# Off-diagonal blocks of the chunk inverses made for two chunks at a time, and new priorities for the mixers

## The chip, the cores and the metric

The kernel runs on one core of a Trainium2 chip. The metric is the device time of one execution in microseconds (us). In the profile PE is TensorE's matrix product, PEld its weight load, DVE is VectorE, ACT ScalarE, POOL GpSimd and SP SyncE, which issues the transfers.

## The reference

One inference step of a decoder trunk of two layers, for a prompt of 16 + 512 rows and 8 sample rows, all in float32. Each layer is a half-step feed-forward block, a mixer and a second half-step feed-forward block:

```python
x = x + 0.5 * _swiglu(_rmsnorm(x, p['norm_ffn1'][l]), p['ffn1_w_in'][l], p['ffn1_w_out'][l])
h, s_w, s_s, s_c = _mixer(_rmsnorm(x, p['norm_mix'][l]), ...)
x = x + h
x = x + 0.5 * _swiglu(_rmsnorm(x, p['norm_ffn2'][l]), p['ffn2_w_in'][l], p['ffn2_w_out'][l])
```

The mixer's core is a recurrence over the rows, per head, with a 64 x 64 state (16 heads), beside a short convolution and two gates:

```python
Sa = jnp.einsum('bhvk,bhk->bhv', S, a_t)
S = S * w_t[:, :, None, :] + Sa[..., None] * b_t[:, :, None, :] + v_t[..., None] * k_t[:, :, None, :]
y = jnp.einsum('bhvk,bhk->bhv', S, r_t)
```

## The kernel before

The 536 columns (528 prompt rows and 8 sample rows) lie along the free dimension, the 1024 features over 8 tiles of 128 partitions. Each large product is split into three float32r products (high by high, high by low, low by high; `mm3`), with the weights split when they are loaded: `raw` by DMA, `hi` by ScalarE, `lo` by VectorE (`load_split`). Their accumulators are called `acc`, `a`, `x`, `y`, `z`, `ag` and `au`.

The mixer takes the recurrence in 11 chunks (NC) of 48 rows (C), for two heads at a time: 8 head pairs p in each layer. In a chunk, a unit lower triangular 48 x 48 matrix is inverted for each head. `stage_k(p)` makes the keys' side: projections, two low-rank products (`lora`), decays with a scan (`cum`), norms (`kq`, `kql`, `wn`), the Gram products (`wg`) and the inverses. The diagonal blocks of 24 rows (HC) are inverted on POOL by 23 steps of two operations (`pr`, `Xinv`) over a tile `Ta`, which comes through DRAM (`td`), and go through DRAM (`xd`) into the tile `Yd`. The off-diagonal block of each chunk is then made on TensorE by three operations of 48 x 48 per chunk: a transpose (w1, lines 1061 to 1077), a product with `off`, the off-diagonal block (w2), and a product with the inverse of the lower block (w3). They go in two halves of 6 and 5 chunks (SPL), each through one PSUM bank (tag c0 or c1 by the pair's parity), with a copy out by ScalarE after every step. The trace calls all of these tiles w: w<-cst,Yd is w1, w<-x,off is w2 and w<-Yd,x is w3. LATE (4 us) delays w1's operations in the plan.

`stage_v(p)` makes the values' side (`wv`, `wg`, `wp`), `chain(p)` steps through the 11 chunks one after the other with five TensorE operations each (all named cq), in the same bank as the pair's inverse, and `gnorm(p)` normalizes (`wm`). `stage_m(p)` and `merged(p)` gate and split the result. `gated_parts` are 40 projections and their elementwise work, which `fill` hands out between the stages by the list `gated`. `sample()` makes the 8 sample rows' recurrence in 8 blocks, each with a state tile in the buffers of `Ta` (line 1335). In the tail of the mixer the first half of the output product (`mh`, `ml`) is made.

All instructions go through a planner (`Sched`), which builds each engine's order when the kernel is built: an operation's priority is its place in the program less the `boost` of its stage (MIX, one set for each layer: k, v, c, g, m, i, s and w for stages, f for gated parts, e for the copies out of projections, h for weight loads ahead). Each has a price by `price` (lines 142 to 161); the planner takes the ready operation of the highest priority. `vector` in MIX lists the elementwise operations that VectorE makes; POOL makes the others. Since every operation is issued by one line, the trace gives L273 for all of them, and they are told apart by their tiles.

Of the kernel before, what the change touches and what calls it, by code (L numbers as in the profile page):

```python
# [7 lines left out]
F32 = mybir.dt.float32  # L8
F32R = mybir.dt.float32r
AF = mybir.ActivationFunctionType  # L10
# [5 lines left out]
P = 128  # L16
# [15 lines left out]
C = 48  # L32
NC = L // C
HC = C // 2
D = 64
# [3 lines left out]
RW = C + D  # L39
NH = 16  # L40

MIX = [dict(boost={'k': 600, 'v': 2000, 'c': 2000, 'g': -1500, 'f': -1000, 'm': -1000, 's': -1000, 'i': 2000, 'w': -6000, 'e': 0, 'h': 0},
            ka=4, gated=[0, 2, 0, 0, 0, 1, 1, 1, 0, 0, 2, 1, 0, 1, 1, 2, 0, 1, 2, 1, 0, 0, 0, 1, 2, 2, 0, 0, 2, 1, 0, 0],
            same=3000, inv=(),
            vector=('bv', 'ka', 'kh', 'kql', 'kt', 'm', 'mb', 'rk', 'rnip', 'rt', 's1', 's3a', 'sl', 'u', 'yl', 'zg')),
       dict(boost={'k': 1500, 'v': -1000, 'c': 2000, 'g': 100, 'f': -3000, 'm': -50, 's': 1000, 'i': 1500, 'w': 50, 'e': -2000, 'h': -2000},
            ka=4, gated=[0, 3, 0, 0, 1, 0, 0, 1, 1, 0, 2, 2, 1, 0, 0, 1, 0, 0, 1, 4, 1, 0, 1, 0, 1, 1, 0, 1, 1, 1, 0, 0],
            same=0, inv=(),
            vector=('bv', 'kh', 'kql', 'kt', 'm', 'mb', 'rk', 'rt', 's3a', 'sl', 'u', 'yl', 'zg'))]
LATE = 4.0  # L50
SHARE = 0.7
FIRST = -300
# [47 lines left out]
class Sched:  # L100
# [41 lines left out]
    def price(self, eng, fn, out, ins, kw):  # L142
        n = self.width(out)
        if fn == "dma_start":
            return 0.48, 4 * n * out.shape[0] / self.DMA_RATE
        if eng == "tensor":
            if fn == "transpose" or kw.get("is_transpose"):
                return n / 1200 + 2e-3, self.HOP
            return (max(n, 256) / 2400 + 12e-3 if ins[0].dtype == F32R else n / 600 + 6e-3), self.HOP
        if eng == "vector":  # L150
            if fn == "memset":
                return 8e-3 + n / 960, self.HOP
            if fn == "reciprocal":
                return 0.12 + n * 6.16e-3, self.HOP
            if fn == "tensor_reduce":
                n = self.width(ins[0])
            return (0.15 if len(ins) > 2 else 0.09) + n / 960, self.HOP
        if eng == "scalar":
            psum = any(x.tensor.space == PSUM for x in ins + [out])
            return (0.05 if psum else 0.095) + (0.09 if "scale" in kw else 0) + n / 1200, self.HOP  # L160
        return (0.28 + n * 1.7e-3 if fn == "tensor_tensor" else 0.2 + n * 1e-3), self.HOP
# [198 lines left out]
class Build:  # L360
# [423 lines left out]
    def mixer(self, l, xh, xl, mD):  # L784
        tc, nc, io, cst, R = self.tc, self.nc, self.io, self.cst, self.R
        V, G, A, T, S = nc.vector, nc.gpsimd, nc.scalar, nc.tensor, nc.sync
# [3 lines left out]
        boost, ka = opt['boost'], opt['ka']  # L790
        self.ahead = boost['h']
        E = lambda n: V if n in opt['vector'] else G
        with ExitStack() as ctx:
# [19 lines left out]
            o, _ = _PC["mu"]  # L813
            V.tensor_scalar(out=omu, in0=self.par[l][:, o:o + 26], scalar1=-1.0, scalar2=1.0, op0=ALU.mult, op1=ALU.add)
            nkk = pp.tile([P, 8], F32, name="nkk")
            o, _ = _PC["kk"]
# [41 lines left out]
            for i in range(2):  # L858
                t = pp.tile([P, NC, 2 * C], F32, name=f"Yd{i}")
                G.memset(t, 0.0)  # L860
                yds.append(t)
            off = pp.tile([P, NC, C], F32, name="off")
            G.memset(off, 0.0)

            def mname(c):
                return "mask" if c % 2 == 0 else "mask2"
# [71 lines left out]
            def stage_k(p):  # L938
# [91 lines left out]
                for g in range(4):  # L1030
                    S.dma_start(out=td[g].rearrange("c s t -> s c t"), in_=GT[g * HC:(g + 1) * HC])
                NP, HJ = 88, HC // 2
                Ta = pp.tile([P, HC, HC], F32, tag="Ta", name="Ta", bufs=2)
                for q in range(2):
                    for b in range(2):
                        o = (2 * q + b) * 22
# [17 lines left out]
                    rw = slice(g * HC, (g + 1) * HC)  # L1054
                    S.dma_start(out=Yd[rw, :, rw], in_=xd[g].rearrange("c j t -> j c t"))
                for h in range(2):
                    rw = slice(h * HC, (h + 1) * HC)
                    S.dma_start(out=off[rw, :, rw], in_=td[h, :, :, HC:].rearrange("c s t -> s c t"))
                    S.dma_start(out=Yd[rw, :, C + h * HC:C + (h + 1) * HC], in_=xd[2 + h].rearrange("c j t -> j c t"))

                for c0, c1 in SPL:
                    n = c1 - c0
                    x1, x2 = (pp.tile([P, 6 * C], F32, tag="tH", name=t, bufs=3)[:C, :n * C].rearrange("p (c q) -> p c q", c=n)
                              for t in ("x1", "x2"))

                    def step(fn, out, name):
                        w = psp.tile([P, 512], F32, tag=f"c{p % 2}", name=name, bufs=1)
                        for i in range(n):
                            fn(w[:C, i * C:(i + 1) * C], c0 + i)
                        A.activation(out=out, in_=w[:C, :n * C].rearrange("p (c q) -> p c q", c=n), func=AF.Copy)  # L1070

                    nc.pad = LATE
                    step(lambda o, c: T.transpose(o, Yd[:C, c, :C], cst["id"][:C, :C]), x1, "w1")
                    nc.pad = 0.0
                    step(lambda o, c: T.matmul(out=o, lhsT=off[:C, c, :], rhs=x1[:, c - c0, :], start=True, stop=True), x2, "w2")
                    step(lambda o, c: T.matmul(out=o, lhsT=x2[:, c - c0, :], rhs=Yd[:C, c, C:], start=True, stop=True),
                         Yd[:C, c0:c1, C:], "w3")

                nc.boost = boost['k']
                kf, kh, rk = a, k, r  # L1080
# [193 lines left out]
            def sample():  # L1274
# [57 lines left out]
                bv_ = lambda i: VB[:, i, :].unsqueeze(1).to_broadcast([P, SV, D])  # L1332
                for q in range(D // SV):
                    vs = slice(q * SV, (q + 1) * SV)
                    stf = pp.tile([P, HC * HC], F32, tag="Ta", name="s2", bufs=2)[:, :SV * D]
                    st = stf.rearrange("p (a b) -> p a b", a=SV)
                    S.dma_start(out=stf, in_=io["swkv"][l][:, q * SV * D:(q + 1) * SV * D])
                    t1 = tmp("t1")[:, :SV * D].rearrange("p (a b) -> p a b", a=SV)
                    E('s1').tensor_tensor(out=t1, in0=st, in1=bv_(3), op=ALU.mult)
                    V.tensor_reduce(out=sa[:, vs], in_=t1, op=ALU.add, axis=AX.X)  # L1340
                    E('sw').tensor_tensor(out=st, in0=st, in1=bv_(0), op=ALU.mult)
                    t2 = tmp("t2")[:, :SV * D].rearrange("p (a b) -> p a b", a=SV)
                    E('s2').tensor_tensor(out=t2, in0=bv_(4), in1=sa[:, vs].unsqueeze(2).to_broadcast([P, SV, D]), op=ALU.mult)
                    E('s2a').tensor_tensor(out=st, in0=st, in1=t2, op=ALU.add)
                    t3 = tmp("t3")[:, :SV * D].rearrange("p (a b) -> p a b", a=SV)
                    E('s3').tensor_tensor(out=t3, in0=bv_(1), in1=VB[:, 2, vs].unsqueeze(2).to_broadcast([P, SV, D]), op=ALU.mult)
                    E('s3a').tensor_tensor(out=st, in0=st, in1=t3, op=ALU.add)
                    S.dma_start(out=io["o_sswkv"][l][:, q * SV * D:(q + 1) * SV * D], in_=stf)
                    t4 = tmp("t4")[:, :SV * D].rearrange("p (a b) -> p a b", a=SV)
                    E('s4').tensor_tensor(out=t4, in0=st, in1=bv_(5), op=ALU.mult)  # L1350
                    V.tensor_reduce(out=y[:, vs], in_=t4, op=ALU.add, axis=AX.X)
# [267 lines left out]
```

## Time and profile before

| | us |
|---|---|
| median of 3 runs | 2955.64 (2954.28 to 2958.29) |
| the profiled execution | 2957.18 |
| its span, first to last instruction | 2955.4 |

| engine | busy us | share of the span |
|---|---|---|
| PE | 2873.6 | 97% |
| PEld | 2811.0 | 95% |
| DVE | 2135.9 | 72% |
| ACT | 1362.6 | 46% |
| POOL | 587.7 | 20% |

The feed-forward blocks take the span from 0 to 390, from 1110 to 1840 and from 2575 on; the mixers lie between them. A busy PE contains records that overlap: what a group of records costs is read from the starts of the records before and behind it, not from their durations.

### The profile page before, as it was taken

What the parts mean: (1) busy time and instruction counts of PE and PEld (TensorE: products, weight loads), DVE (VectorE), ACT (ScalarE), POOL (GpSimd) and SP (SyncE); (2) the same over time, 40 slices, a digit from 0 to 9 for tenths busy, and PEclk for the clock granted to TensorE, in tenths of its full rate; (3) what the DMA queues carried; (4) which work ended last, traced back from release to release, by engine and by line L of the source; (5) the groups of instructions that cost most, each with busy time, mean ns of one, the idle gap of its engine ahead of it and who ended that gap; (6) DMA issues with size and microseconds to landing.
All of it is one profiled execution on the core that took longest, in us unless ns stands there. A gap on an engine that the chain in (4) does not pass through costs nothing.

```text
span 2955.4 us, 57453 instructions
## 1 busy us (share of the span) xinstructions
PE 2873.6 (97%) x23026; PEld 2811.0 (95%) x23026; DVE 2135.9 (72%) x3995; ACT 1362.6 (46%) x2284; POOL 587.7 (20%) x1120
## 2 busy tenths in 40 slices
PE   8999999999999899999999999999999999999998
PEld 8999999999999899999999999999899998899997
DVE  8677767677776968676687766667766768687775
ACT  5444454344444245444454444535454442554444
POOL 1000026222342800000100001343430428100001
PEclk9999999999999989999999999999999999999999
DMA  3223323232323362323323333232232234623332
GB/s 133 93 96 98 112 87 92 74 86 83 87 64 99 130 207 87 104 90 104 108 71 101 100 94 116 90 96 78 62 84 75 62 103 139 214 79 108 96 102 80
DMA packets 219516, 294.22 MB, mean 100 GB/s; under 512 B 119824, under 2 KB 128784, under 8 KB 219248
## 3 DMA queue, kind: packets, MB, share of 16 engines
q1 hardware_dynamic: 219248, 290.54, 32.0%
q8 instruction: 181, 2.97, 0.4%
q14 instruction: 87, 0.71, 0.1%
HBM read 256.38 MB, written 34.10 MB: 98 GB/s over the span
## 4 chain that ended last, share of the span: by engine, by line
PE 86%; DVE 6%; ACT 2%; DMA 2%; issue 2%; POOL 1%; SPq 0%; DVEq 0%; ACTq 0%; POOLq 0%
PE acc L273 26%; PE a L273 17%; PE x L273 13%; PE y L273 7%; PE cq L273 5%; PE wg L273 3%; PE au L273 3%; PE z L273 3%; PE ag L273 3%; PE w L273 2%; DVE lo L273 2%; PE wp L273 2%; DMA raw<-in_f_in 1%; ACT hi L273 1%; POOL t L273 1%
## 5 line engine op out<-in xcount | busy, mean ns | idle before, releaser
L273 ACT ACTIVATE hi<-raw 128x1024 fp32r<-128x1024 f32 (+4 forms) x460 | 388.5, 845 | 488.6 <-PE acc L273 190.4
L273 DVE TENSOR_TENSOR lo<-raw,hi 128x1024 fp32r<-128x1024 f32 (+4 forms) x460 | 449.3, 978 | 58.0 <-ACT hi L273 52.2
L273 PE MATMUL acc<-xh,hi 128*128 128x268 f32 (+1 forms) x2112 | 481.3, 301 | 6.8 <-ACT sig L273 2.2
L273 PE MATMUL acc<-xh,lo 128*128 128x268 f32 (+1 forms) x2112 | 482.3, 301 | 5.5 <-DVE lo L273 5.4
L273 PE MATMUL acc<-xl,hi 128*128 128x268 f32 (+1 forms) x2112 | 478.2, 299 | 0.0
L273 PEld LDWEIGHTS acc<-xh,hi 128*128 128x128 f32 x2112 | 343.6, 192 | 12.5 <-ACT sig L273 3.3
L273 PEld LDWEIGHTS acc<-xh,lo 128*128 128x128 f32 x2112 | 343.6, 192 | 10.9 <-DVE lo L273 8.8
L273 PEld LDWEIGHTS acc<-xl,hi 128*128 128x128 f32 x2112 | 343.1, 191 | 1.1
L273 PE MATMUL a<-hh,lo 128*128 128x268 f32 (+1 forms) x1408 | 288.0, 285 | 0.9 <-DVE lo L273 0.9
L273 PE MATMUL a<-hl,hi 128*128 128x268 f32 (+1 forms) x1408 | 287.3, 285 | 0.0
L273 PE MATMUL a<-hh,hi 128*128 128x268 f32 (+1 forms) x1408 | 286.7, 285 | 0.0
L273 POOL MEMSET wide<- 128x104 f32 (+1 forms) x7 | 1.3, 188 | 1327.4 <-DVE s L273 945.8
L273 PE MATMUL x<-xh,hi 128*128 128x268 f32 (+1 forms) x864 | 247.3, 286 | 1.4 <-ACT sn L273 1.2
L273 PE MATMUL x<-xl,hi 128*128 128x268 f32 (+1 forms) x864 | 247.1, 286 | 0.0
L273 PE MATMUL x<-xh,lo 128*128 128x268 f32 (+1 forms) x864 | 246.9, 286 | 0.0
L273 ACT ACTIVATE hi<-s 128x1024 fp32r<-128x1024 f32 x144 | 152.0, 1057 | 185.8 <-DVE s L273 121.8
L273 PEld LDWEIGHTS a<-hh,lo 128*128 128x128 f32 x1408 | 219.6, 188 | 1.1 <-DVE lo L273 1.1
L273 PEld LDWEIGHTS a<-hl,hi 128*128 128x128 f32 x1408 | 218.6, 188 | 0.0
L273 PEld LDWEIGHTS a<-hh,hi 128*128 128x128 f32 x1408 | 218.6, 188 | 0.0
L273 DVE TENSOR_TENSOR lo<-s,hi 128x1024 fp32r<-128x1024 f32 x144 | 174.6, 1220 | 19.6 <-ACT hi L273 18.7
L273 POOL TENSOR_TENSOR pr<-Ta,Xinv 88x22 f32<-88x22 f32 (+16 forms) x368 | 149.6, 407 | 146.9 <-DMA Ta<-td 122.2
L273 DVE SCALAR_TENSOR_TENSOR X<-a,X 128x536 f32<-128x536 f32 (+1 forms) x160 | 113.0, 707 | 74.4 <-PE a L273 74.2
(570 smaller groups left out, 7204.3 us busy)
## 6 DMA issues: line engine op xcount, KB each, us to landing
raw<-in_f_in SPq DMA_DIRECT2D x176, 512.0 KB
raw<-in_w_in SPq DMA_DIRECT2D x132, 512.0 KB
raw<-in_f_out SPq DMA_DIRECT2D x128, 256.0 KB
raw<-in_f_out SPq DMA_DIRECT2D x32, 384.0 KB
raw<-in_w_o SPq DMA_DIRECT2D x32, 256.0 KB
XD<-X SPq DMA_DIRECT2D x16, 268.0 KB
s<-in_swkv SPq DMA_DIRECT2D x16, 256.0 KB
out_o_sswkv<-s SPq DMA_DIRECT2D x16, 256.0 KB
```

The lines of the kernel that those rows point to most:

```text
L273: return getattr(getattr(self.nc, o.eng), o.fn)(*o.args, **o.kw)
```

## The change

The transposes are made for an even chunk and the odd one after it together: the odd chunk's upper inverse stands beside the even one's in `Yd`, so one transpose of 48 x 96 puts the two below each other. `off` becomes block diagonal for two chunks (96 x 96, six of them), so one product of K = 96 makes w2 for both, and a new tile `xb` holds the lower inverses of two chunks as a block diagonal, so one product with 96 moving columns makes w3 for both. The eleventh chunk stays single. w1 and w2 are made for all chunks in one bank, w3 in two halves as before. `xb` and `off` are filled by four transfers each, `Yd`'s second half by two. `Ta` has one buffer instead of two, and the sample's state alternates between it and `xb`.

Beside it the planner's prices of transposes, of small float32 products and of scans change, and in MIX the boosts, the gated counts, layer 1's `same` and which operations VectorE makes. Only blank lines are left out of the changed code:

```diff
--- before.py
+++ after.py
@@ -39,14 +39,14 @@
 RW = C + D
 NH = 16
 
-MIX = [dict(boost={'k': 600, 'v': 2000, 'c': 2000, 'g': -1500, 'f': -1000, 'm': -1000, 's': -1000, 'i': 2000, 'w': -6000, 'e': 0, 'h': 0},
-            ka=4, gated=[0, 2, 0, 0, 0, 1, 1, 1, 0, 0, 2, 1, 0, 1, 1, 2, 0, 1, 2, 1, 0, 0, 0, 1, 2, 2, 0, 0, 2, 1, 0, 0],
+MIX = [dict(boost={'k': 874, 'v': 2000, 'c': 2000, 'g': -1500, 'f': -1000, 'm': -940, 's': -860, 'i': 2131, 'w': -6000, 'e': 1682, 'h': 765},
+            ka=4, gated=[0, 1, 0, 0, 0, 2, 0, 2, 0, 0, 1, 1, 0, 2, 2, 2, 1, 0, 2, 1, 0, 0, 0, 0, 1, 1, 0, 0, 3, 0, 1, 1],
             same=3000, inv=(),
-            vector=('bv', 'ka', 'kh', 'kql', 'kt', 'm', 'mb', 'rk', 'rnip', 'rt', 's1', 's3a', 'sl', 'u', 'yl', 'zg')),
-       dict(boost={'k': 1500, 'v': -1000, 'c': 2000, 'g': 100, 'f': -3000, 'm': -50, 's': 1000, 'i': 1500, 'w': 50, 'e': -2000, 'h': -2000},
-            ka=4, gated=[0, 3, 0, 0, 1, 0, 0, 1, 1, 0, 2, 2, 1, 0, 0, 1, 0, 0, 1, 4, 1, 0, 1, 0, 1, 1, 0, 1, 1, 1, 0, 0],
-            same=0, inv=(),
-            vector=('bv', 'kh', 'kql', 'kt', 'm', 'mb', 'rk', 'rt', 's3a', 'sl', 'u', 'yl', 'zg'))]
+            vector=('ka', 'kh', 'kt', 'm', 'mb', 'rk', 'rnip', 'rt', 's3a', 'sl', 'sw', 'u', 'yl', 'zg')),
+       dict(boost={'k': 1457, 'v': -1000, 'c': 2063, 'g': 100, 'f': -5869, 'm': -1268, 's': 1000, 'i': 1498, 'w': 50, 'e': -2663, 'h': -2000},
+            ka=4, gated=[0, 3, 0, 0, 1, 0, 0, 1, 1, 0, 2, 2, 1, 0, 0, 1, 0, 1, 1, 2, 1, 1, 1, 1, 1, 1, 1, 0, 0, 0, 1, 0],
+            same=3000, inv=(),
+            vector=('bv', 'kh', 'kql', 'kt', 'm', 'mb', 'rk', 'rt', 's3a', 'sl', 'u', 'zg'))]
 LATE = 4.0
 SHARE = 0.7
 FIRST = -300
@@ -145,8 +145,8 @@
             return 0.48, 4 * n * out.shape[0] / self.DMA_RATE
         if eng == "tensor":
             if fn == "transpose" or kw.get("is_transpose"):
-                return n / 1200 + 2e-3, self.HOP
-            return (max(n, 256) / 2400 + 12e-3 if ins[0].dtype == F32R else n / 600 + 6e-3), self.HOP
+                return n / 1200 + 35e-3, self.HOP
+            return (max(n, 256) / 2400 + 12e-3 if ins[0].dtype == F32R else max(n / 600 + 6e-3, 0.14)), self.HOP
         if eng == "vector":
             if fn == "memset":
                 return 8e-3 + n / 960, self.HOP
@@ -154,6 +154,8 @@
                 return 0.12 + n * 6.16e-3, self.HOP
             if fn == "tensor_reduce":
                 n = self.width(ins[0])
+            if fn == "tensor_tensor_scan":
+                n *= 2
             return (0.15 if len(ins) > 2 else 0.09) + n / 960, self.HOP
         if eng == "scalar":
             psum = any(x.tensor.space == PSUM for x in ins + [out])
@@ -859,8 +861,11 @@
                 t = pp.tile([P, NC, 2 * C], F32, name=f"Yd{i}")
                 G.memset(t, 0.0)
                 yds.append(t)
-            off = pp.tile([P, NC, C], F32, name="off")
+            off = pp.tile([P, 6, 2 * C], F32, name="off")
+            xb = pp.tile([P, 6, 2 * C], F32, name="xb")
             G.memset(off, 0.0)
+            G.memset(xb, 0.0)
 
             def mname(c):
                 return "mask" if c % 2 == 0 else "mask2"
@@ -1030,7 +1035,7 @@
                 for g in range(4):
                     S.dma_start(out=td[g].rearrange("c s t -> s c t"), in_=GT[g * HC:(g + 1) * HC])
                 NP, HJ = 88, HC // 2
-                Ta = pp.tile([P, HC, HC], F32, tag="Ta", name="Ta", bufs=2)
+                Ta = pp.tile([P, HC, HC], F32, tag="Ta", name="Ta", bufs=1)
                 for q in range(2):
                     for b in range(2):
                         o = (2 * q + b) * 22
@@ -1054,27 +1059,36 @@
                     rw = slice(g * HC, (g + 1) * HC)
                     S.dma_start(out=Yd[rw, :, rw], in_=xd[g].rearrange("c j t -> j c t"))
                 for h in range(2):
-                    rw = slice(h * HC, (h + 1) * HC)
-                    S.dma_start(out=off[rw, :, rw], in_=td[h, :, :, HC:].rearrange("c s t -> s c t"))
-                    S.dma_start(out=Yd[rw, :, C + h * HC:C + (h + 1) * HC], in_=xd[2 + h].rearrange("c j t -> j c t"))
+                    S.dma_start(out=Yd[h * HC:(h + 1) * HC, 0:NC - 1:2, C + h * HC:C + (h + 1) * HC], in_=xd[h, 1::2].rearrange("c j t -> j c t"))
+                for par in range(2):
+                    n = 6 - par
+                    for h in range(2):
+                        rw = slice(par * C + h * HC, par * C + (h + 1) * HC)
+                        S.dma_start(out=off[rw, :n, rw], in_=td[h, par::2, :, HC:].rearrange("c s t -> s c t"))
+                        S.dma_start(out=xb[rw, :n, rw], in_=xd[2 + h, par::2].rearrange("c j t -> j c t"))
+                x1, x2 = (pp.tile([P, 6 * C], F32, tag="tH", name=t, bufs=3) for t in ("x1", "x2"))
+                kp = lambda i: 2 * C if 2 * i + 1 < NC else C
+                def step(fn, out, name):
+                    w = psp.tile([P, 512], F32, tag=f"c{p % 2}", name=name, bufs=1)
+                    for i in range(6):
+                        fn(w[:kp(i), i * C:(i + 1) * C], i, kp(i))
+                    A.activation(out=out[:2 * C, :5 * C], in_=w[:2 * C, :5 * C], func=AF.Copy)
+                    A.activation(out=out[:C, 5 * C:], in_=w[:C, 5 * C:6 * C], func=AF.Copy)
+                nc.pad = LATE
+                step(lambda o, i, m: T.transpose(o, Yd[:C, 2 * i, :m], cst["id"][:C, :C]), x1, "w1")
+                nc.pad = 0.0
+                step(lambda o, i, m: T.matmul(out=o, lhsT=off[:m, i, :m], rhs=x1[:m, i * C:(i + 1) * C], start=True, stop=True), x2, "w2")
                 for c0, c1 in SPL:
                     n = c1 - c0
-                    x1, x2 = (pp.tile([P, 6 * C], F32, tag="tH", name=t, bufs=3)[:C, :n * C].rearrange("p (c q) -> p c q", c=n)
-                              for t in ("x1", "x2"))
-                    def step(fn, out, name):
-                        w = psp.tile([P, 512], F32, tag=f"c{p % 2}", name=name, bufs=1)
-                        for i in range(n):
-                            fn(w[:C, i * C:(i + 1) * C], c0 + i)
-                        A.activation(out=out, in_=w[:C, :n * C].rearrange("p (c q) -> p c q", c=n), func=AF.Copy)
-                    nc.pad = LATE
-                    step(lambda o, c: T.transpose(o, Yd[:C, c, :C], cst["id"][:C, :C]), x1, "w1")
-                    nc.pad = 0.0
-                    step(lambda o, c: T.matmul(out=o, lhsT=off[:C, c, :], rhs=x1[:, c - c0, :], start=True, stop=True), x2, "w2")
-                    step(lambda o, c: T.matmul(out=o, lhsT=x2[:, c - c0, :], rhs=Yd[:C, c, C:], start=True, stop=True),
-                         Yd[:C, c0:c1, C:], "w3")
+                    w = psp.tile([P, 512], F32, tag=f"c{p % 2}", name="w3", bufs=1)
+                    for c in range(c0, c1, 2):
+                        i, m = c // 2, kp(c // 2)
+                        T.matmul(out=w[:C, (c - c0) * C:(c - c0) * C + m], lhsT=x2[:m, i * C:(i + 1) * C], rhs=xb[:m, i, :m], start=True, stop=True)
+                    A.activation(out=Yd[:C, c0:c1, C:], in_=w[:C, :n * C].rearrange("p (c q) -> p c q", c=n), func=AF.Copy)
 
                 nc.boost = boost['k']
                 kf, kh, rk = a, k, r
@@ -1332,7 +1346,7 @@
                 bv_ = lambda i: VB[:, i, :].unsqueeze(1).to_broadcast([P, SV, D])
                 for q in range(D // SV):
                     vs = slice(q * SV, (q + 1) * SV)
-                    stf = pp.tile([P, HC * HC], F32, tag="Ta", name="s2", bufs=2)[:, :SV * D]
+                    stf = (xb.rearrange("p a b -> p (a b)") if q % 2 else pp.tile([P, HC * HC], F32, tag="Ta", name="s2", bufs=1))[:, :SV * D]
                     st = stf.rearrange("p (a b) -> p a b", a=SV)
                     S.dma_start(out=stf, in_=io["swkv"][l][:, q * SV * D:(q + 1) * SV * D])
                     t1 = tmp("t1")[:, :SV * D].rearrange("p (a b) -> p a b", a=SV)
```

## Rows read from the trace of the kernel before

**Rows 1.** The page, busy time by engine (share of the span, instructions).
```profile
PE 2873.6 (97%) x23026; PEld 2811.0 (95%) x23026; DVE 2135.9 (72%) x3995; ACT 1362.6 (46%) x2284; POOL 587.7 (20%) x1120
```

**Rows 2.** Stretches: length, busy PE, PEld, DVE, ACT, POOL (instructions), granted clock, DMA, GB/s.
```profile
390.00:950.00 560.00, 549.41 (x4443) 529.93 (x4442) 401.39 (x947) 263.17 (x481) 191.45 (x473) 0.99 0.30 83
950.00:1110.00 160.00, 147.18 (x1093) 139.31 (x1092) 124.30 (x242) 59.01 (x121) 66.95 (x56) 0.93 0.50 165
1110.00:1840.00 730.00, 729.59 (x5905) 728.90 (x5904) 537.49 (x804) 346.46 (x524) 18.75 (x15) 1.00 0.31 98
1840.00:2400.00 560.00, 544.87 (x4376) 522.29 (x4375) 392.84 (x932) 270.56 (x487) 193.63 (x479) 0.99 0.29 81
2400.00:2575.00 175.00, 161.04 (x1233) 153.04 (x1233) 128.26 (x245) 63.44 (x129) 79.88 (x67) 0.96 0.48 155
```

**Rows 3.** The same view of one short stretch in the first mixer's tail.
```profile
1031.20:1044.80 13.60, 11.17 (x49) 9.91 (x49) 9.04 (x19) 1.56 (x6) 1.72 (x1) 0.50 0.58 193
```

**Rows 4.** PE's waits over the whole span: us in total, times, longest.
```profile
PE cq L273 <- DVE rd L273: 5.5, 6, 2.6
...
PE wn L273 <- DVE kql L273: 0.3, 1, 0.3
```

**Rows 5.** PE's groups by shape: busy us, mean ns of one, idle before.
```profile
L273 PE MATMUL w<-x,off 48*48 48x48 f32 x352 | 23.2, 209 | 0.0
L273 PE MATMUL w<-Yd,x 48*48 48x48 f32 x352 | 22.9, 209 | 0.0
...
L273 PE MATMUL w<-cst,Yd 48*48 48x48 f32 x176 | 19.2, 210 | 0.0
```

**Rows 6.** Timeline of PE in the first mixer: start, us, records merged.
```profile
485.89 0.41 PE L273 MATMUL acc<-xh,lo 128*128 128x268 f32 x2
486.23 0.22 PE L273 MATMUL w<-cst,Yd 48*48 48x48 f32 x1
486.38 0.51 PE L273 MATMUL acc<-ta,hi 128*128 128x268 f32 x2
...
490.28 0.39 PE L273 MATMUL w<-cst,Yd 48*48 48x48 f32 x5
...
495.78 0.41 PE L273 MATMUL acc<-xl,hi 128*128 128x268 f32 x2
496.13 0.73 PE L273 MATMUL w<-x,off 48*48 48x48 f32 x12
496.79 0.51 PE L273 MATMUL acc<-xh,lo 128*128 128x268 f32 x2
```

**Rows 7.** The same timeline at two other kinds of float32 product.
```profile
394.02 1.17 PE L273 MATMUL ss<-cst,wide 128*128 128x1 f32 x10
...
502.35 1.25 PE L273 MATMUL wg<-mv,BK 128*96 128x160 f32 x8
```

**Rows 8.** PEld's groups by shape: busy us, mean ns of one load, idle before.
```profile
L273 PEld LDWEIGHTS cq<-rd,Yd 96*96 96x96 f32 x352 | 50.0, 166 | 8.2 <-DVE rd L273 7.4
...
L273 PEld LDWEIGHTS w<-x,off 48*48 48x48 f32 x352 | 18.5, 121 | 5.7 <-issue 1.6 <-ACT yh L273 0.3 <-ACT x L273 0.2
```

**Rows 9.** Tile w between 606 and 638 us: duration ns, first and last start.
```profile
L273 PE MATMUL w<-Yd,x x22: 205/205/240, 618.5 to 636.3; 48*48 48x48 f32 x22
...
L273 PE MATMUL w<-cst,Yd x11: 202/203/223, 607.1 to 628.9; 48*48 48x48 f32 x11
```

**Rows 10.** Tile Yd: SP's issue of its transfers, ns min/median/max.
```profile
L273 SPq DMA_DIRECT2D Yd<-xd x96: 290/403/1384, 479.0 to 2382.5; - x96
```

**Rows 11.** SP's own waits: us in total, times, longest.
```profile
SPq L273 <- DVE lo L273: 722.7, 248, 17.3
```

**Rows 12.** Tiles cum and kql, and POOL's groups: ns of one elementwise operation.
```profile
L273 DVE TENSOR_TENSOR_SCAN cum<-cst,sig x16: 1240/1246/1260, 418.7 to 2300.9; 128x528 f32<-128x528 f32 x16
...
L273 DVE TENSOR_TENSOR kql<-kq,kqh x16: 690/709/841, 424.0 to 2306.4; 128x528 fp32r<-128x528 f32 x16
...
L273 POOL TENSOR_TENSOR ka<-k,a 128x528 f32<-128x528 f32 x8 | 10.5, 1317 | 26.0 <-PE wn L273 19.2 <-DVE kql L273 6.7
```

## The prediction

> **What bounds the kernel now.** The page's first part comes first: TensorE is busy 97% of the span [rows 1], so the kernel ends when TensorE has done its work, and an edit pays by taking time out of TensorE or by closing its gaps. The table of stretches says where gaps are [rows 2]. The feed-forward stretch 1110 to 1840 is full (729.59 of 730 us, clock 1.00): nothing can be won there. The gaps lie in the two mixers. Their middles (390 to 950 and 1840 to 2400) leave 560 - 549.41 = 10.6 and 560 - 544.87 = 15.1 us idle; their tails (950 to 1110 and 2400 to 2575), where the last chain, the sample group and the first half of the output product run, leave 12.8 and 14.0 us, and their granted clock is 0.93 and 0.96, worth another 160 x 0.07 = 11.2 and 175 x 0.04 = 7.0 us. The half clock follows TensorE's own gaps: from 1031.2 to 1044.8 it is granted 0.50, the lower of its two levels (1.2 GHz), and 13.60 - 11.17 = 2.4 us are idle in that stretch too [rows 3]. The table of waits over the whole run names small latencies and no single one: the longest sum inside the mixers is cq waiting for rd, 5.5 us in 6 waits [rows 4]. So the bound in both mixers is TensorE's work, with some 45 us of gaps and low clock in the two tails.
>
> **Part 1, the products by two chunks.** Each of the 16 head pairs (8 in each layer) has 11 chunks, and each chunk a transpose (w1) and two products (w2, w3). A float32 product leaves two records, a transpose one: 176 transposes and 2 x 352 records [rows 5]. Their busy time is 19.2 + 23.2 + 22.9 = 65.3 us, which is the ceiling of any direct saving. After the change a pair has 6 transposes, 6 w2 and 6 w3, five of each for two chunks and one for the single last chunk.
>
> The price before, from the order of TensorE's records [rows 6]: the twelve w2 records of six chunks begin at 496.13 and the last ends 0.73 us later; with 0.205 us for one record the cadence is (0.73 - 0.205)/11 = 0.048 us, in which the first step is a little longer; I use 0.045. Of the stream of acc records around them (one each 0.123 us, from 0.246 for two) the last begins at 495.90 and the next at 496.79, so the block costs 496.79 - 495.90 - 0.12 = 0.77 us: 12 x 0.045 and some 0.2 for going in and out. The single transpose at 486.23 agrees: 486.38 - 486.01 - 0.12 = 0.25. The transposes of a half come as one and, 4 us later, the rest (486.23 and 490.28): the first opens its bank, and LATE is counted again for those behind it. So they lie in four blocks a pair. So a pair costs: w1 4 x 0.2 + 11 x 0.045 = 1.30; w2 and w3 each 2 x 0.2 + 22 x 0.045 = 1.39; together 4.08 us, and 16 x 4.08 = 65.3, which is the busy sum above.
>
> The price after is not in the trace, since no record there has 96 weight columns and 48 moving ones. It lies between two rows. **Lower end:** a record keeps its 0.045 whatever its weights are, if their loading is hidden. **Upper end:** the ss records stream a single column behind weights of 128 columns, and ten of them take 1.17 us, (1.17 - 0.25)/9 = 0.10 us each: there the weight load sets the pace [rows 7]. A weight load's own length grows from 121 ns for 48 columns to 166 for 96 [rows 8]. Between 0.045 at 48 columns and 0.10 at 128 a line gives 0.08 at 96; I take that, as it is the same kind of stream as ss. The w3 products have 48 weight columns and 96 moving ones; the wg records with 160 moving columns run at (1.25 - 0.30)/7 = 0.136 [rows 7], and a line from 48 columns gives 0.084 at 96. So after the change: w1 as 1 + 5 transposes 2 x 0.2 + 5 x 0.08 + 0.045 = 0.85; w2 in one block 0.2 + 10 x 0.08 + 2 x 0.045 = 1.09; w3 in two blocks 0.4 + 10 x 0.084 + 2 x 0.045 = 1.33; together 3.27 us. The saving is 4.08 - 3.27 = 0.81 us a pair, **13 us** in all. Half the instructions are thus worth a fifth of the time, since a record of double width takes nearly twice as long; most of the 0.81 comes from three blocks fewer to go in and out of.
>
> The Trainium skill's pages disagree on this. Its page TensorEngine Tiling (Array Packing), Instruction Overhead, gives every matmul a fixed overhead of about 60 cycles, so that one column costs as much as sixty; by that the count decides, and the sum would be nearer to the lower end (24 us). The page TensorE: Matmul & The Clock Gate, LDWEIGHTS, prices a load by its columns, 96 / 1.2 = 80 ns as an estimate; that rule speaks against most of this change's gain, and the ss and weight-load rows bear it out.
>
> **Part 2, the latency of an inverse.** Before, the second half of the chunks begins when the first half has left the bank, so a pair's products last from 607.1 to 636.3, 29 us [rows 9]. The 4 us pads are paid four times; after, two pads and one pass through w1 and w2 remain, and I put the length at some 14 us (half). The products use the bank of the chain two pairs before, so this is 15 us off a loop of two chains. As TensorE is full while that loop runs, it shortens nothing by itself; it lets the last chain start earlier, and so it can close gaps in the tails only.
>
> **Part 3, transfers and buffers.** Per pair 8 small transfers (2 off, 4 + 2 into Yd) become 14: 4 and 2 into Yd, 4 off, 4 xb. At a median of 0.40 us of SP's issue [rows 10] the six more cost 2.4 us in SP's queue, ahead of the weight loads that are queued behind them. Their cover is SP's slack (it waits 722.7 us in 248 waits until lo has been made from a weight tile and frees it [rows 11]) and the weight tiles already loaded; without cover the bound is 16 x 2.4 = 38 us, with it 0. I take 0, because the table of TensorE's waits has no line for a weight transfer. They lie inside the 15 us of part 2. One Ta buffer instead of two lets the next pair's Ta load wait for the inversion on POOL; eight pairs share the 560 us of a mixer's middle, 70 us each, and POOL is busy for a third of them (191.45 and 193.63 us [rows 2]), so inversions seldom touch; I take 0, and at most the few microseconds of one load, off TensorE's path. The sample's state alternates between Ta and xb, so its second block waits for the last w3 of pair 7, which comes earlier now; I take 0, and the bound is the length of an inverse, 29 us, in a step that TensorE doesn't wait for until the output product.
>
> **Part 4, the priorities and the planner's prices.** The planner gives a scan twice its elements (the trace: 1246 ns for 528, against 0.15 + 528/960 = 0.70 by the old price), transposes 33 ns more, and small float32 products at least 0.14 us. The scan's correction is right by the row [rows 12]; the other two stand for the 0.2 us of going in and out. That plans the DVE queue more truly, and the new boosts and gated counts reorder both mixers. Layer 0 moves bv, kql and s1 to POOL and sw to DVE, layer 1 yl to POOL. For one operation of 528 columns that is 1317 ns on POOL (ka) against 709 on DVE (kql) [rows 12]: 0.6 us later each, and 16 x 0.7 us off DVE in layer 0. What the new order does to TensorE's gaps no row shows. Its bounds are all the tails' 45 us on one side, and on the other some 40 us lost, if the middles doubled their gaps and clock loss (10.6 + 15.1 idle and 0.99 of clock, 2 x 5.6). I take 9 us of gain, a fifth of the tails: the 15 us earlier start of part 2 in tails of 160 and 175 us is a tenth, and I give the truer prices as much again.
>
> **Sum.** The profiled execution took 2957.18 us (span 2955.4 and 1.8 around it). 2957.2 - 13 - 9 = 2935.2. The median of the runs lies 1.5 us below the profiled one, so the forecast is **2934 us**, 0.7% faster.
>
> **The rivals.** A difference of 0.2% (5.9 us) is about what a measurement of this kernel can tell from no change.
> First, the weight load is hidden and the count decides: w1 0.4 + 6 x 0.045 = 0.67, w2 0.2 + 12 x 0.045 = 0.74, w3 0.4 + 0.54 = 0.94, 2.35 a pair, so 1.73 saved, 28 us, and with the 9 of the order 2919. For it: the products have always run at 0.045; against it: the ss row. Chance 0.10.
> Second, the order gains much more: with the shorter loop the chains run ahead, and half of all the gaps and low clock of the mixers (45 + 37 us) go: 13 + 41, 2902 to 2920 with 2912 in the middle. For it: the waits are small and scattered, which a planner can shift; against it: they are left over by a planner already. Chance 0.18.
> Third, the change does less than it says: the direct 13 us are won, and the new order loses about as much in new gaps, as the tails are short of float32r work to fill with; 2950 to 2961. Chance 0.15.
> Fourth, slower: POOL becomes the engine that TensorE waits for in layer 0. kql stands there in one queue with an inversion of 46 operations, and wn, in order on TensorE, waits for it with all acc records behind. The price is 0.6 us a pair for the longer operation and up to 3 or 4 us behind inversion steps, and a low-clock stretch of 3.4 us (1.7 lost) after it. The point from which it decides is 22 / 8 = 2.8 us a pair for a loss at all; at 5.5 us a pair it is 44 - 22 = 22 us slower, 2977. For it: POOL already has 191 us of work in the middle of layer 0; against it: wn has waited for kql only 0.3 us [rows 4], and the planner knows POOL's prices. Chance 0.13.
>
> **How the numbers follow.** The forecast (2924 to 2946) has 0.44, the rivals 0.10, 0.18, 0.15 and 0.13. Faster by over 0.2% are the forecast and the first two: 0.72; within 0.2% 0.15; slower 0.13. The range reaches from 2908, which takes in most of the second rival, to 2960, which takes in the third, and leaves out the fourth and an edge of the second.
>
> **What would show it.** The w records: 96 transposes, 192 w2 and 192 w3; the cadence of w2 and w1 near 0.08 (right) or 0.045 (first rival), of w3 near 0.084; their busy sum near 52 us. An inverse from its first transpose to its last w3 near 14 us. TensorE's idle time in the tails below 27 us and clocks above 0.93 and 0.96. The forecast is wrong if wn waits for POOL, if a line for weight transfers appears among TensorE's waits, or if the feed-forward stretches change at all.

## The result, and the profile after

| | before | after |
|---|---|---|
| median, us | 2955.29 (2954.28 to 2958.29) | 2936.99 (2934.94 to 2941.81) |
| the profiled execution's span, us | 2955.4 | 2933.1 |

The ratio is 0.9939, 95% interval 0.9922 to 0.9956: 0.6% faster, 18 us where 22 were forecast, inside the range. The two profiled executions lie 22.3 us apart, and the stretches below are theirs. They are now cut at the mixers' own ends (length, busy PE, PEld, DVE, ACT, POOL, granted clock, DMA share, GB/s), first before and then after:

```profile
390.10:1115.30 725.20, 701.79 (x5576) 674.45 (x5576) 530.86 (x1192) 325.75 (x607) 260.47 (x530) 0.98 0.35 102
1849.00:2580.00 731.00, 701.91 (x5576) 671.34 (x5575) 520.61 (x1176) 333.94 (x614) 274.22 (x546) 0.98 0.34 100
```
```profile
390.30:1096.60 706.30, 684.85 (x5376) 661.90 (x5375) 527.47 (x1176) 325.85 (x610) 284.39 (x547) 1.00 0.37 104
1832.60:2558.00 725.40, 694.61 (x5377) 665.35 (x5376) 519.99 (x1144) 326.45 (x611) 290.55 (x579) 0.98 0.35 101
```

Layer 0's mixer is 18.9 us shorter, layer 1's 5.6; the feed-forward blocks together are 2.2 us longer. Two hundred records went in each mixer. To tell work from gaps, each mixer's length is split three ways from the trace: idle time (length less TensorE's busy time), clock loss (half of the time at the lower clock), and the rest, called work below. The table gives this for both mixers together, in us, each from the kernel's one profiled execution. The experiments' ratios are to the kernel before as it was measured along with them, at 2957.8 to 2959.1 us:

| kernel | median of all (ratio to before) | idle | clock loss | work | changes of tile size |
|---|---|---|---|---|---|
| before | 2955.3 | 52.5 | 29.1 | 1374.7 | 291 |
| after | 2937.0 (0.9939) | 52.3 | 17.1 | 1362.3 | 211 |
| e1 products alone | 2970.8 (1.0037) | 71.5 | 32.4 | 1360.3 | 205 |
| e2 order alone | 2964.2 (1.0019) | 61.4 | 13.6 | 1387.8 | 306 |
| e3 prices alone | 2994.0 (1.0120) | 70.4 | 39.3 | 1381.1 | 299 |
| e6 products and prices | 2983.2 (1.0075) | 74.0 | 39.3 | 1362.7 | 217 |
| n1 before, LATE 4.5 | 2964.6 (1.0023) | 55.0 | 25.6 | 1379.9 | 293 |
| n2 before, LATE 3.5 | 2990.4 (1.0105) | 69.7 | 47.8 | 1371.3 | 297 |
| n3 after, LATE 4.5 | 2942.9 (0.9947) | 60.1 | 11.9 | 1364.2 | 207 |
| e10 after, kql on VectorE | 2955.9 (0.9996) | 65.2 | 18.8 | 1368.6 | 217 |
| e9 after, xb loaded twice | 2939.5 (0.9932) | 56.6 | 20.5 | 1355.5 | 218 |
| e8 after, two passes | 2932.3 (0.9904) | 41.8 | 6.8 | 1374.0 | 273 |
| e7 after, full width | 2929.3 (0.9895) | 49.0 | 11.9 | 1361.0 | 116 |
| e12 e7 in layer 0, e8 in layer 1 | 2922.5 (0.9877) | 47.1 | 3.4 | 1369.1 | 194 |

The last column counts neighbouring TensorE records (starts less than about 0.4 us apart) of which one has at most 48 weight rows, or at most 48 weight columns, where the other has 96 or 128. Between before and after the work fell by 12.4 us and idle time and clock loss by 12.2. The new products, by PE's groups of the changed kernel (busy us, mean ns of one; idle before):

```profile
L275 PE MATMUL w<-xb,x 96*48 96x96 f32 x160 | 20.2, 254 | 0.0
L275 PE MATMUL w<-x,off 96*96 96x48 f32 x160 | 16.5, 246 | 0.6 <-ACT x L275 0.6
L275 PE MATMUL w<-cst,Yd 48*96 48x48 f32 x80 | 10.1, 222 | 0.0
L275 PE MATMUL w<-x,off 48*48 48x48 f32 x32 | 4.6, 223 | 0.2 <-ACT x L275 0.2
L275 PE MATMUL w<-xb,x 48*48 48x48 f32 x32 | 4.6, 222 | 0.0
L275 PE MATMUL w<-cst,Yd 48*48 48x48 f32 x16 | 3.2, 203 | 0.0
```

The counts are the forecast's: 96 transposes, 192 and 192 records [rows 5]; the groups' busy times sum to 59.2 us against 65.3, where the forecast had 52. These records overlap their neighbours, so what they cost is read from starts, in PE's timeline of the changed kernel (start, us):

```profile
495.20 0.41 PE L275 MATMUL acc<-xl,hi 128*128 128x268 f32 x2
495.54 0.43 PE L275 MATMUL w<-cst,Yd 48*96 48x48 f32 x5
495.90 0.51 PE L275 MATMUL acc<-xh,lo 128*128 128x268 f32 x2
...
504.68 0.27 PE L275 MATMUL wv<-cst,v 128*96 128x128 f32 x1
504.79 1.19 PE L275 MATMUL w<-x,off 96*96 96x48 f32 x12
505.90 0.42 PE L275 MATMUL wv<-cst,v 128*96 128x128 f32 x2
...
506.90 0.70 PE L275 MATMUL w<-xb,x 96*48 96x96 f32 x6
507.52 0.78 PE L275 MATMUL wg<-mv,BK 128*96 128x160 f32 x4
```

Less the last record's own length (0.205 us for 48 x 48, 0.246 for w3) the cadences are (0.43 - 0.205)/4 = 0.056 us for w1, (1.19 - 0.205)/11 = 0.090 for w2 with one break in it and (0.70 - 0.246)/5 = 0.091 for w3. The first step of a block is longer: over the whole run the median from one record's start to the next is 0.048 us in w1, 0.085 between w2's 96 x 96 records and 0.083 in w3. And w2 is entered 0.11 us after a record of `wv`, so without the 0.1 us that a block of w cost on entry before [rows 6].

### The profile page after: what moved, and what is told of

Same layout as the page of the kernel before. It is cut to its first block, busy times and chain, and to the rows that moved or that the text cites. A ratio compares the mean times of both kernels' runs of the same rounds, so it can differ in the third digit from the quotient of the medians.

```text
span 2933.1 us, 56821 instructions
## 1 busy us (share of the span) xinstructions
PE 2849.5 (97%) x22626; PEld 2791.7 (95%) x22626; DVE 2132.5 (73%) x3947; ACT 1353.1 (46%) x2284; POOL 628.2 (21%) x1170
## 4 chain that ended last, share of the span: by engine, by line
PE 84%; DVE 7%; ACT 3%; DMA 2%; POOL 2%; issue 2%; SPq 0%; DVEq 0%; ACTq 0%; POOLq 0%
PE acc L275 24%; PE a L275 17%; PE x L275 13%; PE y L275 7%; PE cq L275 5%; PE z L275 3%; PE au L275 3%; PE wg L275 3%; PE ag L275 3%; DVE lo L275 2%; PE w L275 2%; PE wp L275 2%; DMA raw<-in_f_in 1%; POOL t L275 1%; ACT hi L275 1%
## 5 line engine op out<-in xcount | busy, mean ns | idle before, releaser
L275 PE MATMUL acc<-xh,lo 128*128 128x268 f32 (+1 forms) x2112 | 475.2, 299 | 5.3 <-DVE lo L275 5.2
L275 POOL TENSOR_TENSOR pr<-Ta,Xinv 88x22 f32<-88x22 f32 (+16 forms) x368 | 141.3, 384 | 135.3 <-DMA Ta<-td 107.3
L275 DVE SCALAR_TENSOR_TENSOR X<-a,X 128x536 f32<-128x536 f32 (+1 forms) x160 | 112.9, 705 | 70.6 <-PE a L275 70.4
```

The source lines that it names most:

```text
L275: return getattr(getattr(self.nc, o.eng), o.fn)(*o.args, **o.kw)
```

## The experiments

**One part at a time.** Two kernels take one part each: e1 has the new products with MIX and `price` of before, e2 the products of before with the new MIX and `price`.

> The products for two chunks with their transfers and tiles, but the planner's prices and the mixers' boosts, gated counts and engine choices of the kernel before. Theory A (the products are worth 13 us by themselves, and the order adds to it): 2942 us, within 2937 to 2947. Theory B (the gain is the order's, and the products alone only move gaps about): 2950 to 2960.

> The kernel before with the changed kernel's prices, boosts, gated counts and engine choices, its products still made chunk by chunk. Theory A: the order is worth the remaining 5 to 9 us, 2946 to 2950. Theory B (the order carries the gain): 2935 to 2941. A third case: the order was found for the changed products and costs time without them, 2956 or more.

Measured: e1 2970.8 us, ratio 1.0037 (1.0024 to 1.0049); e2 2964.2, 1.0019 (1.0009 to 1.0029). Both parts alone are slower, e2 by no more than the prediction calls no change, and together they are 0.6% faster. Neither theory had that for e1; e2 is the third case. The two mixers of e1, by the same view of stretches:

```profile
389.50:1131.80 742.30, 704.85 (x5376) 676.07 (x5375) 532.12 (x1192) 327.05 (x609) 257.24 (x531) 0.97 0.35 99
1871.20:2593.30 722.10, 687.97 (x5376) 662.38 (x5376) 525.78 (x1176) 329.15 (x612) 277.80 (x547) 0.99 0.35 101
```

The work fell as forecast (1374.7 to 1360.3, 14 us), layer 1 became 8.9 us shorter than before, but layer 0 became 17.1 longer: 742.3 - 704.85 = 37.4 us idle instead of 23.4, and a clock of 0.97. The saving was there and was lost again in gaps.

**The planner's prices.** e3 is the kernel before with the new `price`, e6 the changed kernel with MIX of before.

> The kernel before with the planner's new prices alone (scans, transposes, small float32 products). If truer prices help by themselves (the prediction gave them half of 9 us): 2949 to 2952. If the priorities of before fit the old prices: 2956 or more.

> The changed kernel with the old boosts, gated counts and engine choices: products and prices, no new priorities. Theory A with prices worth 4 us: 2938. If only the priorities carry what the products don't: like the products alone, 2942.

Measured: e3 2994.0, 1.0120 (1.0099 to 1.0140); e6 2983.2, 1.0075 (1.0056 to 1.0094). Neither of e6's expectations held. Truer prices with the old boosts cost 1.2%: of the 36 us between the profiled executions 28 are gaps and clock, 6 work. With these prices and boosts the same in both, the products bring 10.8 us (e6 against e3), and 18.4 us of work.

**Is it the order as such?** After e1 a new theory was needed, C: a set of boosts fits one plan, and whatever makes the planner order anew opens gaps. Two kernels differ from before, and one from after, by a single number of the plan:

```diff
-LATE = 4.0
+LATE = 4.5
```

> The kernel before with one number of the plan changed: the transposes' delay LATE is 4.5 us instead of 4.0. No instruction is added, removed or moved to another engine. Theory C (the boosts of a kernel fit one plan, and any edit that makes the planner order anew opens gaps of 10 to 40 us in the mixers, which is why the products alone came out slower): 2965 to 2995 us, TensorE's work in the mixers as before. Theory D (the products with their transfers and copies open those gaps themselves): within 2952 to 2960.

> The same kernel before with LATE 3.5 us. Theory C: 2965 to 2995, and another figure than with 4.5, as the gaps are an accident of the order. Theory D: within 2952 to 2960.

> The changed kernel with LATE 4.5 us and nothing else. Theory C: 2947 to 2977, that is the changed kernel's own order is as much an accident. Theory D: 2935 to 2941, and the shorter loop of two chains makes the plan sturdy.

Measured: n1 2964.6, 1.0023 (1.0014 to 1.0032); n2 2990.4, 1.0105 (1.0089 to 1.0120); n3 2942.9, 0.9947 (0.9932 to 0.9962). No instruction differs between n2 and before, and it is 32 us slower; its stretches:

```profile
389.00:1139.50 750.50, 710.00 (x5576) 679.78 (x5575) 534.33 (x1192) 329.16 (x608) 258.97 (x530) 0.97 0.34 98
1873.20:2611.50 738.30, 709.12 (x5577) 677.84 (x5576) 523.70 (x1176) 336.23 (x615) 274.46 (x546) 0.97 0.33 99
```

So C holds for n2; n1 moved by 0.2%, just below C's range and above D's, and n3 lies between the two expectations. The products needn't be at fault for e1's gaps: a harmless edit does as much. Taken over all orders, the five kernels with single chunks have 1371.3 to 1387.8 us of work (mean 1379.0) and the six with pairs in one pass and of the same width 1355.5 to 1368.6 (mean 1362.3): every one of these is below every one of those, 17 us on average.

The blocks of w can also be priced by themselves in every trace, free of the order's gaps: from the start of the record before a block to that of the record behind it, less the usual step of the record before (0.123 us for acc), as the median of each kind of block (by step and number of records, without idle time, at full clock) times their number. They cost 68.4 to 69.9 us in the five kernels with single chunks and 54.0 to 55.2 in the six with pairs: 14 us less, in any order.

**POOL's kql, the fourth rival.**

```diff
-vector=('ka', 'kh', 'kt', 'm', 'mb', 'rk', 'rnip', ...
+vector=('ka', 'kh', 'kql', 'kt', 'm', 'mb', 'rk', 'rnip', ...
```

> The changed kernel with kql made on VectorE again in layer 0 (8 operations of 128x528). If TensorE's wn waits for POOL there (the prediction's fourth rival, at a smaller price): 2925 to 2934, with no wait of wn or of what follows it. If POOL's kql is covered, as no wait of wn shows in the changed kernel, only the order changes: by theory C 2945 to 2975, by theory D 2935 to 2941.

Measured: 2955.9, 0.9996 (0.9985 to 1.0006). Giving kql back costs 19 us, all in layer 0 (727.3 us; layer 1 stays at 725.4 as in the changed kernel), 15 of them idle time. That is theory C's range: what the new order costs hides what kql itself is worth. In the changed kernel wn never waited for POOL; its only line among PE's waits (us, times, longest) is

```profile
PE wn L275 <- ACT kqh L275: 0.3, 1, 0.3
```

though kql does take longer there, by tile kql of the changed kernel (ns min/median/max; layer 0 on POOL, layer 1 on DVE):

```profile
L275 POOL TENSOR_TENSOR kql<-kq,kqh x8: 1307/1320/1812, 424.3 to 829.4; 128x528 fp32r<-128x528 f32 x8
L275 DVE TENSOR_TENSOR kql<-kq,kqh x8: 693/709/811, 1866.6 to 2286.3; 128x528 fp32r<-128x528 f32 x8
```

**The shorter inverse.** e8 makes w1, w2 and w3 in two passes again, still for two chunks at a time (the calls alone are shown; the copies are split to match):

```diff
-                step(lambda o, i, m: T.transpose(...), x1, "w1")
-                step(lambda o, i, m: T.matmul(out=o, lhsT=off[:m, i, :m], ...), x2, "w2")
                 for c0, c1 in SPL:
+                    i0, i1 = c0 // 2, (c1 + 1) // 2
+                    step(lambda o, i, m: T.transpose(...), x1, "w1", i0, i1)
+                    step(lambda o, i, m: T.matmul(out=o, lhsT=off[:m, i, :m], ...), x2, "w2", i0, i1)
```

> The changed kernel with w1, w2 and w3 made in two passes over chunks 0 to 5 and 6 to 10, as before, but still for two chunks at a time. It takes away the single pass alone. An inverse from first transpose to last w3 goes from 19 back to 27 to 30 us, and the blocks more cost 0.3 to 0.5 us a pair, 5 to 8 us of TensorE's work. If the shorter loop of two chains matters for the gaps, the idle time and low clock of the mixers rise as well: 2955 to 2980. If it doesn't, only the work and the accident of the order show: 2942 to 2965.

Measured: 2932.3, 0.9904 (0.9882 to 0.9926), below both ranges. Tile w in a window of one inverse (ns, first and last start), first of the changed kernel, then of e8:

```profile
L275 PE MATMUL w<-xb,x x12: 205/246/283, 636.7 to 639.3; 96*48 96x96 f32 x10, 48*48 48x48 f32 x2
...
L275 PE MATMUL w<-cst,Yd x6: 203/207/246, 620.1 to 624.9; 48*96 48x48 f32 x5, 48*48 48x48 f32 x1
```
```profile
L275 PE MATMUL w<-xb,x x12: 205/246/284, 632.9 to 650.0; 96*48 96x96 f32 x10, 48*48 48x48 f32 x2
...
L275 PE MATMUL w<-cst,Yd x6: 203/244/244, 621.2 to 643.3; 48*96 48x48 f32 x5, 48*48 48x48 f32 x1
```

An inverse takes 650.0 - 621.2 = 29 us again instead of 19 (medians of the 16 pairs: 28.4 and 18.5), the blocks of w cost 62.2 us, some 8 more, and the work rose by 11.7 us, yet idle time and clock loss fell from 69.4 to 48.6 us. So few gaps need no single pass; what the pass is worth to the gaps one order can't tell.

**More transfers.** e9 issues the four transfers into xb twice, for every pair.

> The changed kernel with the four transfers into xb issued twice (18 small transfers a pair instead of 14). The prediction took nothing for such transfers, with 0.4 us of SP's issue each as the bound, 16 x 1.6 = 26 us. If SP's queue has that slack: no wait for weight transfers among TensorE's waits, work unchanged at 1360 to 1369, total by the accident of the order 2937 to 2960. If the transfers push the weight loads: waits of TensorE for raw or lo rise in the mixers, 2960 or more.

Measured: 2939.5, 0.9932 (0.9914 to 0.9949), the changed kernel's time within the intervals; the work, 1355.5 us, lies a little below what was expected. PE's waits for split weights, lo and hi, by acc (us, times, longest) are, first after, then e9:

```profile
PE acc L275 <- DVE lo L275: 5.2, 9, 1.0
...
PE acc L275 <- ACT hi L275: 1.1, 2, 0.9
```
```profile
PE acc L275 <- DVE lo L275: 7.0, 13, 1.2
...
PE acc L275 <- ACT hi L275: 2.8, 2, 2.5
```

No line for a weight's transfer appears in either, and the waits for split weights rose by 3.5 us. In the kernel before the same two sum to 9.2. So four more transfers a pair show as 2 to 4 us, in this one order, not as 26.

**Full width.** Where does a block's 0.2 us come from? e7 leaves no small product in w2 and in the first five w3:

```diff
-                kp = lambda i: 2 * C if 2 * i + 1 < NC else C
+                kp = lambda i: 2 * C
...
-                    A.activation(out=out[:2 * C, :5 * C], in_=w[:2 * C, :5 * C], func=AF.Copy)
-                    A.activation(out=out[:C, 5 * C:], in_=w[:C, 5 * C:6 * C], func=AF.Copy)
+                    A.activation(out=out[:2 * C, :], in_=w[:2 * C, :6 * C], func=AF.Copy)
...
-                        T.matmul(out=w[:C, ...], lhsT=x2[:m, i * C:(i + 1) * C], rhs=xb[:m, i, :m], start=True, stop=True)
+                        q = min(6 - i, 2) * C
+                        T.matmul(out=w[:q, ...], lhsT=x2[:m, i * C:i * C + q], rhs=xb[:m, i, :m], start=True, stop=True)
```

> The changed kernel with the single last chunk padded to a pair (transpose, w2 and w3 take 96 rows and columns there, w2's copy is one) and with 96 weight columns instead of 48 for the first five w3 (the extra output rows are never read). Theory S (a block of w costs its extra 0.2 us because TensorE changes between products of over 64 rows and columns and products of 48, some 0.09 us in and 0.09 out): the twelve w2 records run at 0.085 us without a break, w2 and most w3 blocks are entered and left at no cost, and TensorE's work in both mixers (busy time less what the low clock takes) falls from 1362 to 1356 to 1359 us although more columns are loaded. If the 0.2 us belongs to float32 against float32r products, the blocks stay as dear and the work rises by 1 to 3 us. The total moves with the new order besides, 2928 to 2965.

Measured: 2929.3, 0.9895 (0.9874 to 0.9917). PE's timeline of e7:

```profile
500.31 0.28 PE L275 MATMUL acc<-xh,hi 128*128 128x268 f32 x1
500.43 1.14 PE L275 MATMUL w<-x,off 96*96 96x48 f32 x12
501.39 0.37 PE L275 MATMUL acc<-xh,hi 128*128 128x268 f32 x1
501.60 0.41 PE L275 MATMUL acc<-xl,hi 128*128 128x268 f32 x2
```

w2 follows an acc record after 0.12 us, like another acc record; in [rows 6] it was 0.23. A w2 block of 12 records costs 0.98 us here and 1.12 in the changed kernel (medians of 13 and 10 blocks, priced as above), although two of its records are wider. The changes of tile size fell from 211 to 116. So a float32 product as such is entered for nothing, and the change of tile size costs. All blocks of w cost 49.4 us, 5 less than the changed kernel's 54.5, which is what theory S expected of the work. The work itself fell by 1.3 us only, and between two orders of one program it moves by more than that. The one copy also shortens an inverse, to 14.0 us (median). What part of e7's 8 us in the total is the width and what the order's luck stays open.

**Both better halves.** e12 has e7's products in layer 0 and e8's passes in layer 1.

> Full-width products in one pass in layer 0 and the two passes in layer 1: the better order of each layer put together. If a layer's plan doesn't depend on the other layer's (a change in layer 0 alone left layer 1 at 725.4 us, as in the changed kernel), the mixers take 706 and 712.5 us, and the kernel 2929 - 3.4 = 2926 us, within 2921 to 2931. If layer 1's plan depends on when layer 0 ends, layer 1 comes out anywhere between 712 and 740, and the kernel up to 2950.

Measured: 2922.5, 0.9877 (0.9855 to 0.9898), the fastest of all: 1.2% below before, and some 14 us below the changed kernel. The mixers took 706.2 and 713.5 us, as each layer's plan had in its own kernel (706.1 and 712.5).

## Why the prediction was right, and where its steps failed

**The bound.** Right. TensorE stayed at 97%, the feed-forward blocks moved by 2 us (the prediction allowed none; over the other kernels they are 1 us shorter to 12 longer than before), and all else happened in the mixers.

**Part 1, 13 us.** Right in size: 14 us in the blocks of w, 12.4 us of work between the two profiles, 14.4 in e1, 17 over all orders. Its terms were off both ways. By pair w1 costs 0.72 us, not 0.85, w2 1.11 where 1.09 was forecast, and w3 1.57, not 1.33; before the three were 4.29, not 4.08, as some blocks are split. That 16 x 4.08 equals the busy sum was chance. w1 steps by 0.048 us, not by 0.08: a transpose loads its weights faster, which `wv` (a transpose) showed in the trace of before, 127 ns for 96 columns against 166 for the product in [rows 8]; I priced it by the wrong neighbour:

```profile
L273 PEld LDWEIGHTS wv<-cst,v 128*96 128x96 f32 x176 | 21.1, 127 | 0.8
```

w2's 0.085 and w3's 0.083 stand against 0.08 and 0.084. In w2 the moving columns stayed at 48 while the weights grew from 48 x 48 to 96 x 96, so there the weights set the pace, and the first rival (0.045, 28 us; the prediction's 24 us for the same case has no working) is out. The 0.2 us of a block was read rightly but put down to going in and out as such; e7 shows that it belongs to the change of tile size. w3's blocks pay it at both ends, w2's where they fall to 48 x 48 and at their end.

**Part 2.** The mechanism failed twice. First, an inverse takes 19 us, not 14. The sum left two pads, but `step` makes two copies out of w1 while `nc.pad` is LATE, and the plan sets the second behind the first by one more pad. So w2 waits through three, here by PE's and ScalarE's timelines of the changed kernel:

```profile
620.08 0.24 PE L275 MATMUL w<-cst,Yd 48*96 48x48 f32 x1
624.72 0.43 PE L275 MATMUL w<-cst,Yd 48*96 48x48 f32 x5
629.69 0.35 ACT L275 ACTIVATE x<-w 96x240 f32<-96x240 f32 x1
634.21 0.19 ACT L275 ACTIVATE x<-w 48x48 f32<-48x48 f32 x1
634.50 1.22 PE L275 MATMUL w<-x,off 96*96 96x48 f32 x12
```

e7, which makes one copy, takes the forecast's 14.0 us. Second, no order here has gaps that follow this length: idle time and clock loss are 69.4 us at 18.5 us an inverse, 60.9 at e7's 14.0 and 48.6 at e8's 28.4. The tails' idle time went up, not down, in the same windows as [rows 2] from 26.8 to 32.0 us (in the last 160 and 175 us of the two mixers from 26.7 to 31.6):

```profile
950.00:1110.00 160.00, 145.72 (x1101) 138.99 (x1101) 124.27 (x227) 66.71 (x123) 65.05 (x52) 0.98 0.52 171
2400.00:2575.00 175.00, 157.31 (x1183) 149.36 (x1182) 132.09 (x228) 74.57 (x134) 81.91 (x69) 0.95 0.52 168
```

What was won is the clock of layer 0: its clock loss fell from 15.4 to 3.4 us, most of it in the tail (0.93 to 0.98). Layer 1's stayed at 13.7, and its tail's clock, 0.95, isn't above the 0.96 that was to show it.

**Part 3, nothing.** Right as far as one order shows it: e9 adds four transfers a pair and stays within the changed kernel's time.

**Part 4, 9 us.** The figure was met (12.2 us of gaps and clock less the 2.2 in the feed-forward blocks), by luck: as a term of its own it is wrong. By themselves the new prices cost 35 us, and the new prices and priorities 5. The products cost 12 us under the old prices and priorities (e1), and win 11 under the new prices alone (e6 against e3) and some 25 under both (after against e2). The terms don't add, because each order's gaps are its own. The bounds given for the order, 45 us of gain and 40 of loss, were the right size: n2's one number moved 32 us. The truer prices, to which I gave half of the gain, gain nothing by themselves; the scan's price alone was not tried.

**The rivals.** The second (half of all gaps and low clock go) didn't come: 81.6 us became 69.4. e12's order comes nearer, with 50.5. The third (the order eats the saving) is what e10 did, and e1 overshot it; it deserved more than 0.15. The fourth (POOL's kql) is out, as wn never waits for POOL.

## What to carry to other kernels

When a planner lays out the whole order, price an edit by the engine's work, and treat the gaps as a draw that an edit makes anew (changing LATE alone moved these kernels by at most 6 us twice and by 32 once): change a number that does nothing, two or three times, before a difference of 1% is put down to an edit. Compare the work, in which the edit shows through every order, and choose the order for the edited program; here layers planned apart could be chosen apart (e12). Keep small products at the tile size of their neighbours, even if half of their columns are waste: it took 5 us off the blocks of w. Look for delays that a plan counts more than once.

## What the runs showed of the hardware that I had not expected

- Going from a product of 96 or 128 weight rows and columns to one with 48 of either costs about 0.09 us, and so does going back: 0.23 against 0.12 us from the acc record to w2 in [rows 6], nothing in e7, and 0.18 instead of 0.085 inside the changed kernel's w2 block where it goes from 96 x 96 to 48 x 48. The step from 48 x 96 to 48 x 48 inside w1 is free, 0.048 us like its other steps. The Trainium skill, page TensorEngine Tiling (Array Packing), Key Properties, says that a change of the tiling mode drains TensorE; the traces show a cost that fits this, and no more of it than the cost.
- The weight load of a float32 transpose is faster than that of a float32 product of as many columns, 123 ns against 167. Its 48 rows are not the reason: the transpose `wv` has 128 rows and takes 127 ns in the kernel before. PEld's groups of the changed kernel (busy us, mean ns):

```profile
L275 PEld LDWEIGHTS w<-x,off 96*96 96x96 f32 x160 | 16.0, 167 | 1.1 <-ACT x L275 1.0
...
L275 PEld LDWEIGHTS w<-cst,Yd 48*96 48x96 f32 x80 | 6.1, 123 | 4.9 <-issue 1.6 <-DMA raw<-in_w_in 0.2
```
